# Second parts of the projection weights in a two-block transformer: computed on VectorE instead of GpSimd

## Chip, cores and metric

The kernel runs on one core of a Trainium2 chip. The metric is the device time of one execution in microseconds (us), the median of three runs of the same program. Engines are named as the profile names them: PE is TensorE (PEld its weight loads), DVE is VectorE, ACT is ScalarE, POOL is GpSimd, SP is SyncE, which here only issues DMAs. Names such as L129 are lines of the kernel before the change; the changed kernel has one line less from L394 on and two less from L1443 on, so its L470 is L471 of the kernel before.

## What is computed

Two transformer blocks over 1024 tokens of width 1024, all in float32. Cut to what matters here:

```python
def first_block(x, mem, ...):
    y = rmsnorm(h, norm_mix_g) @ w_in             # 1024 x 2560: q, k, v (512 each), conv a and g (512 each)
    att = dilated_sliding_attention(rotary(q), rotary(k), v)
    conv = conformer_conv(a, g, conv_w, ...)      # a * sigmoid(g), 31 taps per channel, layernorm, silu
    h = h + concat(att, conv) @ w_out
    ...                                           # cross attention to mem, then an MLP of 4096
def second_block(x, ...):
    z = rms_norm(x, ln1_g) @ w_in + b_in          # 1024 x 5632: q, k, v, u, y_branch, two gates
    ...                                           # neighbourhood attention; conv of 4 taps and a linear
    ...                                           # recurrence (RG-LRU) in two directions on u; MLP of 4096
```

## The kernel before

**Products in two parts.** PE multiplies in a reduced float32 form, so each float32 operand is kept as two parts. `split` (L125) makes them: ACT rounds the source into the first part `hi` (L128), and a subtraction makes the second part `lo` as source less `hi` (L129). A product is then three matmuls: hi by hi, hi by lo, lo by hi (L177 to L179 in `mm3`, L206 in `gemm_s`).

**Weights of the projections.** `w_s` (L139) fetches one chunk of 256 columns of a weight in two halves of 512 rows. Each half is a DMA of 512 KB on SP's queue (L148) into a tile `raw`, then a split into two tiles `w` of 128x1024. There are two `raw` buffers and twelve `w` buffers, so three chunks of `w` are held, and a third `raw` load waits until the `lo` of the first has been computed. The attribute `b.wlo` says who computes `lo` of these weights: `self.split(hi, lo, raw, eng=self.wlo)` at L154, where None means DVE.

**Block 1, `mix_part` (L389).** In the order of the program: the inputs are normed and transposed into `xT` (x scaled on DVE at L293, transposed on PE at L240, split at L131 and L132); then the chunks for the gate g and for a of the convolution, two halves of them (PE L206), whose product u is written by DVE (L448); then v in two chunks (n = 0 and 1) of eight 128-token tiles each, 24 matmuls of 128x256 for a tile; then q and k in four chunks. A tile of v leaves its PSUM bank by an ACT copy (L470) into a tile `t2k`, of which there are four, and goes to DRAM by an SP DMA (L471). The 31 taps of the convolution are DVE instructions on 128x1024 (L422, 30 for each of four channel groups); they stand in a background list, and `b.pump` takes some of them into the program after each tile of v (L472) and each half of a q/k chunk (L511). A scheduler then fixes one order of instructions for each engine ahead of the run, by readiness in its own model and by priority; on the chip each engine and each DMA queue works through its list in order.

**Block 2, `block2` (L1436).** Chunks of the branches y, u, q/k, v and of four gates, in a fixed list; for each of eight channel groups the background list has the small convolution, the gates and the recurrence in two directions, mostly DVE instructions on 128x1024 (L1439, L1438, L1592 to L1606). The second half of the tokens is normed at its start (L1388 to L1408, in `Front`).

**What the change touches.** L394 sets `b.wlo` to GpSimd at the start of `mix_part`, L1443 does so at the start of `block2`; each is set back to None at the end of the projections (L547, L1645). So GpSimd computes `lo` for 10 chunks in block 1 (20 tiles: g and a twice each, v twice, q/k four times) and 17 in block 2 (34 tiles). All other splits of the kernel are on DVE already.

Of the kernel before, what the change touches and what calls it, by code (L numbers as in the profile page):

```python
# [388 lines left out]
def mix_part(b):  # L389
    nc, i = b.nc, b.i  # L390
    w_in = i["w_in"][0]
    b.xk_d = b.dram.tile([4, P, 2, 2, 256], F32, name="xk_d")
    b.xv_d = b.dram.tile([4, P, 2, 2, 256], F32, name="xv_d")
    b.wlo = nc.gpsimd  # L394
    xc = i["x"][0].rearrange("(l c) d -> c l d", c=4)
    raw = [b.slot(16 + t, name="x") for t in range(NT)]
    load = lambda t: nc.sync.dma_start(out=raw[t], in_=xc[t // 2, (t % 2) * P : (t % 2 + 1) * P, :])
# [1038 lines left out]
def block2(b, h, front):  # L1436
    nc, i = b.nc, b.i
# [2 lines left out]
    turns = front.rest(h)  # L1440
    xT = front.xT

    b.wlo = nc.gpsimd  # L1443
    w_in = i["w_in_2"][0]
    b.v2_d = b.dram.tile([S, 512], F32, name="v2_d")
    b.qk2_d = b.dram.tile([4, 4, P, S], F32, name="qk2_d")
# [370 lines left out]
def build(tc, ins, out, stop=None):  # L1817
    with ExitStack() as ctx:
        b = Builder(tc, ctx, ins, out)
        b.ident = b.cpool.tile([P, P], F32, name="ident")  # L1820
        make_identity(b.nc, b.ident)
        h = mix_part(b)
        if stop not in ("mix",):
            cross_part(b, h)
        if stop not in ("mix", "cross"):
            front = Front(b)
            h = ff_part(b, h, b.g_mlp, ins["w_up"][0], ins["w_down"][0], bias_tables(b), front.work)
            b.layout(None)
        if stop not in ("mix", "cross", "ff"):
            block2(b, h, front)  # L1830
            h = merge_part(b)
        if stop is None:
            h = ff_part(b, h, b.g_ln2, ins["w_ff1_2"][0], ins["w_ff2_2"][0])
            gl = b.slot(26, name="gl")
            b.nc.sync.dma_start(out=gl, in_=ins["lnf_g_2"].partition_broadcast(P))
            final_norm(b, h, gl, out)
        else:
            for t in range(NT):
                b.nc.sync.dma_start(out=out[0, t * P : (t + 1) * P, :], in_=h[t])
# [70 lines left out]
```

## Time and profile before

| what | value |
|---|---|
| median of three runs | 3015.11 us (3013.32 to 3016.35) |
| the profiled execution | 3015.72 us, its span 3013.9 us |
| PE busy | 2895.5 us, 96% of the span |
| DVE busy | 2162.4 us, 72% |
| ACT busy | 1227.5 us, 41% |
| POOL busy | 379.2 us, 13%, of which L129 has 172.7 us in 54 instructions |
| mean granted PE clock | 0.984 of full speed |

The profile names for each instruction the engine, the line, the tiles written and read and their shape. In a row of a timeline, "x7" joins seven instructions in a row, and what stands in brackets is the idle time of that engine just ahead of the row and what ended it. SPq is SP's DMA queue. Busy time of an instruction includes the time in which it waits for data after it has started.

### The profile page before, as it was taken

The numbers are of one execution on the slowest core, as the hardware profiler recorded it, in microseconds if no ns is written. First come the engines' busy times: TensorE is split into PE (matmuls) and PEld (weight loads), VectorE is DVE, ScalarE is ACT, GpSimd is POOL, SyncE is SP. The second block draws the span as 40 slices with busy tenths as digits, with TensorE's granted clock in tenths as the row PEclk, the third lists the DMA queues.
The fourth block names the chain that finished last, engine by engine and source line by source line (L and its number), as shares of the span: only waits on it lengthen the run. The fifth ranks groups of instructions, "written<-read, shape, count | busy, mean of one in ns | idle before, by whom it ended". The sixth has DMA issues, their size and how long they took to land.

```text
span 3013.9 us, 40030 instructions
## 1 busy us (share of the span) xinstructions
PE 2895.5 (96%) x14596; PEld 2438.7 (81%) x14596; DVE 2162.4 (72%) x3889; ACT 1227.5 (41%) x2256; POOL 379.2 (13%) x411
## 2 busy tenths in 40 slices
PE   7899899999999999999999999999999999999997
PEld 5798788788887788888787788898788878888886
DVE  6997787565487776997658777554344776669976
ACT  4122566242253222444655655454211532224444
POOL 2440110000012331000021222200000011100000
PEclk9999899999999999999999999999999999999999
DMA  3135664311124767653231333567842233366522
GB/s 128 49 92 160 178 188 135 99 43 43 50 105 143 230 213 282 246 188 105 72 109 52 101 101 113 174 193 236 281 143 81 98 112 112 109 255 237 182 91 84
DMA packets 251733, 422.86 MB, mean 140 GB/s; under 512 B 27893, under 2 KB 129808, under 8 KB 251536
## 3 DMA queue, kind: packets, MB, share of 16 engines
q1 hardware_dynamic: 213040, 304.29, 31.5%
q0 software_dynamic: 30416, 101.33, 9.7%
q10 hardware_dynamic: 8080, 14.69, 1.3%
q8 instruction: 115, 1.88, 0.3%
q14 instruction: 82, 0.67, 0.1%
HBM read 310.75 MB, written 111.69 MB: 140 GB/s over the span
## 4 chain that ended last, share of the span: by engine, by line
PE 78%; DVE 9%; DMA 5%; ACT 3%; issue 2%; POOL 2%; SPq 1%; DVEq 0%; ACTq 0%; POOLq 0%
PE fd L1182 19%; PE mm L206 18%; PE ff L1009 15%; PE mm L177 5%; PE mm L179 5%; PE mm L178 5%; PE ff L992 2%; PE pv L668 2%; PE tp L734 2%; POOL w L129 1%; PE pv L1708 1%; PE tp L240 1%; DMA bt<-rpb_d 1%; ACT w L128 1%; DVE w L129 1%
## 5 line engine op out<-in xcount | busy, mean ns | idle before, releaser
L1182 PE MATMUL fd<-part,part 128*128 128x512 f32 x2688 | 616.0, 390 | 1.0 <-DVE part L129 1.0
L1182 PEld LDWEIGHTS fd<-part,part 128*128 128x128 f32 x2688 | 504.2, 188 | 110.4 <-DVE part L129 5.8
L1009 PE MATMUL ff<-x,w 128*128 128x512 f32 x2352 | 541.7, 392 | 13.8 <-ACT w L128 7.5
L1009 PEld LDWEIGHTS ff<-x,w 128*128 128x128 f32 x2352 | 443.7, 189 | 111.4 <-ACT w L128 9.2
L206 PE MATMUL mm<-xh,w 128*128 128x512 f32 x1792 | 530.7, 393 | 0.3 <-ACT lruC L1580 0.3
L206 PEld LDWEIGHTS mm<-xh,w 128*128 128x128 f32 x1792 | 336.9, 189 | 68.8 <-ACT lruC L1580 1.4
L128 ACT ACTIVATE part<-keep 128x512 fp32r<-128x512 f32 x384 | 223.8, 623 | 249.5 <-PE fd L1182 243.5
L206 PE MATMUL mm<-xl,w 128*128 128x512 f32 x896 | 316.1, 393 | 0.0
L129 DVE TENSOR_TENSOR part<-keep,part 128x512 fp32r<-128x512 f32 x384 | 250.0, 687 | 44.6 <-ACT part L128 43.9
L128 ACT ACTIVATE w<-raw 128x1024 fp32r<-128x1024 f32 (+1 forms) x132 | 134.9, 1033 | 273.5 <-PE mm L178 111.7
L129 POOL TENSOR_TENSOR w<-raw,w 128x1024 fp32r<-128x1024 f32 x54 | 172.7, 3202 | 444.7 <-ACT w L128 422.5
L206 PEld LDWEIGHTS mm<-xl,w 128*128 128x128 f32 x896 | 168.9, 189 | 33.8 <-issue 0.4
L232 DVE TENSOR_TENSOR h<-h,mm 128x512 f32<-128x512 f32 x176 | 119.8, 686 | 78.6 <-PE mm L179 78.0
L422 DVE SCALAR_TENSOR_TENSOR acc<-u,conv_wh,acc 128x1023 f32<-128x1023 f32 (+14 forms) x120 | 171.7, 1471 | 3.1 <-ACT acc L417 1.3
L177 PE MATMUL mm<-w,xh 128*128 128x256 f32 x512 | 147.9, 289 | 13.5 <-ACT t2k L470 10.3
L852 DVE TENSOR_TENSOR t2k<-ff,t2k 128x512 f32<-128x512 f32 x140 | 96.4, 688 | 82.5 <-PE ff L1009 81.1
L178 PE MATMUL mm<-w,xh 128*128 128x256 f32 x512 | 146.7, 287 | 0.0
L179 PE MATMUL mm<-w,xl 128*128 128x256 f32 x512 | 146.6, 286 | 0.0
L128 ACT ACTIVATE w<-wr 128x512 fp32r<-128x512 f32 x156 | 94.3, 630 | 119.2 <-PE ff L1009 55.5
L974 POOL DMA_DIRECT2D hid_d<-t2k x128 | 70.0, 547 | 489.2 <-DVE t2k L852 265.1
L129 DVE TENSOR_TENSOR w<-raw,w 128x1024 fp32r<-128x1024 f32 (+1 forms) x78 | 91.6, 1180 | 50.2 <-ACT w L128 50.1
L129 DVE TENSOR_TENSOR w<-wr,w 128x512 fp32r<-128x512 f32 x156 | 104.5, 687 | 15.4 <-ACT w L128 14.0
(362 smaller groups left out, 5160.0 us busy)
## 6 DMA issues: line engine op xcount, KB each, us to landing
hid_d<-t2k POOLq DMA_DIRECT2D x128, 256.0 KB, 2.9
x<-hid_d SPq DMA_DIRECT2D x128, 256.0 KB, 4.7
keep<-hid_d SPq DMA_DIRECT2D x96, 256.0 KB, 6.0
raw<-in_w_in_dram SPq DMA_DIRECT2D x38, 512.0 KB, 3.8
qk_d<-t2k SPq DMA_DIRECT2D x64, 256.0 KB, 2.5
wr<-in_w_up_dram SPq DMA_DIRECT2D x32, 512.0 KB, 4.0
keep<-in_w_down_dram SPq DMA_DIRECT2D x64, 256.0 KB, 5.3
wr<-in_w_ff_dram SPq DMA_DIRECT2D x32, 512.0 KB, 3.7
```

The lines of the kernel that those rows point to most:

```text
L128: nc.scalar.activation(hi, src, AF.Copy)
L129: (eng or nc.vector).tensor_tensor(out=lo, in0=src, in1=fp(hi), op=ALU.subtract)
L177: nc.tensor.matmul(ps, sh, mh, start=(i == 0), stop=False)
L178: nc.tensor.matmul(ps, sh, ml, start=False, stop=False)
L179: self.last = nc.tensor.matmul(ps, sl, mh, start=False, stop=(i == n - 1))
L206: self.last = nc.tensor.matmul(pj[j], a, b, start=(k == 0 and q == 0), stop=(k == nk - 1 and q == 2))
L232: self.added[t] = self.nc.vector.tensor_tensor(out=hs, in0=hs, in1=ps, op=ALU.add)
L422: nc.vector.scalar_tensor_tensor(out=acc[m][:, lo:hi], in0=u[m][:, lo + d : hi + d], scalar=w(k), in1=acc[m][:, lo:hi], op0=ALU.mult, op1= ...
L852: tt = lambda o, x, y, op: nc.vector.tensor_tensor(out=o, in0=x, in1=y, op=op)
L974: stored.append(nc.gpsimd.dma_start(out=hid[2 * c + f, :, j * 512 : (j + 1) * 512], in_=o))
L1009: b.last = nc.tensor.matmul(ps, l[:, k, :], r, start=(opens and k == 0 and q == 0), stop=(k == 3 and q == 2), skip_group_check=True)
L1182: last = nc.tensor.matmul(ps[q], l[:, sl], r, start=(c == 0 and x == 0), stop=(c == C - 1 and x == 2))
```

## The change

The two lines that hand the second parts to GpSimd are taken out, so that `b.wlo` stays None and DVE does those subtractions too. GpSimd keeps its DMA issues, its memsets and the casts of the attention.

```diff
@@ mix_part
     b.xk_d = b.dram.tile([4, P, 2, 2, 256], F32, name="xk_d")
     b.xv_d = b.dram.tile([4, P, 2, 2, 256], F32, name="xv_d")
-    b.wlo = nc.gpsimd
     xc = i["x"][0].rearrange("(l c) d -> c l d", c=4)
@@ block2
     xT = front.xT
 
-    b.wlo = nc.gpsimd
     w_in = i["w_in_2"][0]
```

The scheduler makes new lists from this. Outside three stretches (the start, block 1 from its v on, and the projections of block 2) the lists of all engines are the same, and PE's list differs in the start alone.

SP's list in block 1, from the second load of v's second chunk (raw_1247) on; raw_1512 to raw_1791 are the loads of the first two q/k chunks, v_d the stores of v. Before:

```order
L148 DMA raw_1247<-in_w_in_dram 128x4x256
L148 DMA raw_1512<-in_w_in_dram 128x4x128 x2
L148 DMA raw_1519<-in_w_in_dram 128x4x128 x2
L148 DMA raw_1784<-in_w_in_dram 128x4x128 x2
L148 DMA raw_1791<-in_w_in_dram 128x4x128 x2
L471 DMA v_d<-t2k_1008 128x256
L471 DMA v_d<-t2k_1040 128x256
```

After the change:

```order
L148 DMA raw_1247<-in_w_in_dram 128x4x256
L470 DMA v_d<-t2k_1008 128x256
L470 DMA v_d<-t2k_1040 128x256
L470 DMA v_d<-t2k_1072 128x256
L470 DMA v_d<-t2k_1106 128x256
L470 DMA v_d<-t2k_1138 128x256
L470 DMA v_d<-t2k_1170 128x256
L148 DMA raw_1512<-in_w_in_dram 128x4x128 x2
L470 DMA v_d<-t2k_1202 128x256
L148 DMA raw_1519<-in_w_in_dram 128x4x128 x2
```

The loads of two q/k chunks stood ahead of every store of v; now six stores come first and the loads stand between the later ones.

DVE's list in block 1 behind the last u of the convolution (u_799 from mm_937), which before is followed by 42 taps and then by the rotation of q and k:

```order
L448 SCALAR_TENSOR_TENSOR u_799<-th_798,mm_937 128x2x256
L422 SCALAR_TENSOR_TENSOR acc_640<-u_429,conv_wh,acc_640 128x1012
L422 SCALAR_TENSOR_TENSOR acc_1076<-u_483,conv_wh,acc_1076 128x1022
L422 SCALAR_TENSOR_TENSOR acc_640<-u_429,conv_wh,acc_640 128x1011
L422 SCALAR_TENSOR_TENSOR acc_1076<-u_483,conv_wh,acc_1076 128x1021
```

After the change 14 taps follow u_799, and then the two second parts of v's second chunk (w_1244 and w_1250):

```order
L421 SCALAR_TENSOR_TENSOR acc_1076<-u_483,conv_wh,acc_1076 128x1018
L421 SCALAR_TENSOR_TENSOR acc_640<-u_429,conv_wh,acc_640 128x1009
L421 SCALAR_TENSOR_TENSOR acc_1076<-u_483,conv_wh,acc_1076 128x1017
L129 TENSOR_TENSOR w_1244<-raw_1241,w_1243 128x1024
L421 SCALAR_TENSOR_TENSOR acc_1076<-u_483,conv_wh,acc_1076 128x1016
L129 TENSOR_TENSOR w_1250<-raw_1247,w_1249 128x1024
L421 SCALAR_TENSOR_TENSOR acc_1076<-u_483,conv_wh,acc_1076 128x1015
```

From the first tap up to w_1244 DVE's list has 61 rows: 52 taps, 5 writes of u and 4 other second parts. Behind w_1250 it has 14 taps up to the first second part of the first q/k chunk.

DVE's list at the start of block 2, in the chain of small instructions that norms the second half of the tokens (sm_13954 to sm_13956). Before:

```order
L248 TENSOR_SCALAR sm_13954<-sm_13955 128x4
L249 TENSOR_TENSOR sm_13955<-sm_13954,sm_13956 128x4
L249 TENSOR_TENSOR sm_13955<-sm_13955,sm_13954 128x4
L259 SCALAR_TENSOR_TENSOR sm_13954<-sm_13955,sm_13954 128x4
L249 TENSOR_TENSOR sm_13955<-sm_13954,sm_13956 128x4
L249 TENSOR_TENSOR sm_13955<-sm_13955,sm_13954 128x4
```

After the change:

```order
L248 TENSOR_SCALAR sm_13954<-sm_13955 128x4
L129 TENSOR_TENSOR w_14087<-raw_14084,w_14086 128x1024
L249 TENSOR_TENSOR sm_13955<-sm_13954,sm_13956 128x4
L249 TENSOR_TENSOR sm_13955<-sm_13955,sm_13954 128x4
L1438 SCALAR_TENSOR_TENSOR gy_14010<-t2k_14037,t2k_14036 128x512
L259 SCALAR_TENSOR_TENSOR sm_13954<-sm_13955,sm_13954 128x4
L249 TENSOR_TENSOR sm_13955<-sm_13954,sm_13956 128x4
L249 TENSOR_TENSOR sm_13955<-sm_13955,sm_13954 128x4
L129 TENSOR_TENSOR w_14330<-raw_14326,w_14329 128x1024
```

Two second parts of weights (w_14087 and w_14330) now stand inside the chain.

## Rows read from the trace of the kernel before

**Rows 1.** The page, part 1: each engine's busy time, its share, and its instructions.
```profile
PE 2895.5 (96%) x14596; PEld 2438.7 (81%) x14596; DVE 2162.4 (72%) x3889; ACT 1227.5 (41%) x2256; POOL 379.2 (13%) x411
```
**Rows 2.** Instructions of L129: durations in ns, least, median and longest.
```profile
L129 DVE TENSOR_TENSOR w<-raw,w x78: 676/1222/1748, 321.6 to 2300.2; 128x1024 fp32r<-128x1024 f32 x70, 128x512 fp32r<-128x512 f32 x8
...
L129 POOL TENSOR_TENSOR w<-raw,w x54: 2353/2601/20462, 12.4 to 1911.1; 128x1024 fp32r<-128x1024 f32 x54
```
**Rows 3.** Busy time by stretch: length, PE, PEld, DVE, ACT, POOL, PE clock, DMA.
```profile
120.00:180.00 60.00, 50.68 (x372) 49.18 (x371) 59.97 (x46) 12.57 (x20) 37.69 (x5) 0.91 0.17 51
...
1580.00:1640.00 60.00, 58.06 (x249) 47.42 (x248) 55.63 (x54) 39.08 (x47) 5.86 (x3) 0.97 0.11 37
```
**Rows 4.** Timeline of PE, block 1: start, duration, line, count, idle before.
```profile
138.14 0.45 PE L177 MATMUL mm<-w,xh 128*128 128x256 f32 x1 [3.06 <-DVE u L448]
...
149.03 0.58 PE L177 MATMUL mm<-w,xh 128*128 128x256 f32 x1 [6.25 <-ACT t2k L470]
...
151.76 0.38 PE L177 MATMUL mm<-w,xh 128*128 128x256 f32 x1
151.97 0.28 PE L178 MATMUL mm<-w,xh 128*128 128x256 f32 x1
152.09 0.28 PE L179 MATMUL mm<-w,xl 128*128 128x256 f32 x1
...
186.32 0.58 PE L177 MATMUL mm<-w,xh 128*128 128x256 f32 x1 [4.09 <-ACT t2k L470]
```
**Rows 5.** Timeline of ACT, v of block 1.
```profile
143.16 1.06 ACT L128 ACTIVATE w<-raw 128x1024 fp32r<-128x1024 f32 x1 [13.02 <-DMA raw<-in_w_in_dram]
...
185.90 0.37 ACT L470 COPY t2k<-mm 128x256 f32<-128x256 f32 x1 [14.72 <-DMA v_d<-t2k]
```
**Rows 6.** Waits of SP's DMA queue, 100 to 200 us: total, times, longest.
```profile
SPq L148 <- POOL w L129: 84.8, 7, 49.4
```
**Rows 7.** Timeline of POOL, v of block 1.
```profile
128.79 13.86 POOL L129 TENSOR_TENSOR w<-raw,w 128x1024 fp32r<-128x1024 f32 x2 [39.34 <-ACT w L128]
...
161.75 23.74 POOL L129 TENSOR_TENSOR w<-raw,w 128x1024 fp32r<-128x1024 f32 x2 [11.33 <-ACT w L128]
```
**Rows 8.** Timeline of DVE, the convolution of block 1.
```profile
74.54 17.30 DVE L422 SCALAR_TENSOR_TENSOR acc<-u,conv_wh,acc 128x1009 f32<-128x1009 f32 x7 [1.31 <-ACT acc L417]
...
104.32 10.79 DVE L422 SCALAR_TENSOR_TENSOR acc<-u,conv_wh,acc 128x1021 f32<-128x1021 f32 x9
...
137.00 1.08 DVE L448 SCALAR_TENSOR_TENSOR u<-th,mm 128x512 f32<-128x512 f32 x1
137.91 68.49 DVE L422 SCALAR_TENSOR_TENSOR acc<-u,conv_wh,acc 128x1012 f32<-128x1012 f32 x43
```
**Rows 9.** Timeline of DVE, the start.
```profile
40.95 2.34 DVE L248 TENSOR_SCALAR sm<-sm 128x2 int32<-128x2 int32 x1
```
**Rows 10.** Timeline of PE, the start.
```profile
44.72 0.44 PE L240 MATMUL tp<-ident,x 128*128 128x128 f32 x2 [2.05 <-DVE xl L132]
```
**Rows 11.** Timeline of DVE, block 2.
```profile
1503.12 1.23 DVE L1388 TENSOR_TENSOR h<-h,gf 128x1024 f32<-128x1024 f32 x1 [1.66 <-ACT junk L1387]
...
1507.10 2.98 DVE L1388 TENSOR_TENSOR h<-h,gf 128x1024 f32<-128x1024 f32 x1 [2.15 <-ACT junk L1387]
...
1879.44 1.22 DVE L1438 TENSOR_TENSOR lruC<-lruC,lruA 128x1024 f32<-128x1024 f32 x1
...
1889.51 3.42 DVE L1438 TENSOR_TENSOR lruC<-lruC,lruA 128x1024 f32<-128x1024 f32 x1
```
**Rows 12.** Timeline of PE, block 2.
```profile
1524.07 0.33 PE L240 MATMUL sc<-ident,h 128*128 128x128 f32 x1 [0.94 <-DVE h L1408]
...
1616.09 0.65 PE L177 MATMUL mm<-w,w 128*128 128x512 f32 x1 [1.94 <-ACT lruA L1580]
...
1657.54 0.80 PE L177 MATMUL mm<-w,w 128*128 128x512 f32 x1 [2.79 <-ACT t2k L1471]
```
**Rows 13.** Timeline of ACT, block 2.
```profile
1655.85 1.06 ACT L128 ACTIVATE w<-raw 128x1024 fp32r<-128x1024 f32 x1 [2.29 <-DMA raw<-in_w_in_dram]
```

## The prediction

> **What bounds the kernel now.** I read the page's busy times first. PE works 2895.5 us, 96% of the span [rows 1], so an edit on other engines can win only where PE idles or runs at a low clock, and can lose wherever its new owner makes PE wait. Then I read the groups of L129: the same 128x1024 subtraction takes DVE 1.222 us in the median, and GpSimd between 2.353 and 20.462 us [rows 2]. Next come the stretches. Between 120 and 180 us DVE is busy 59.97 us of 60, PE only 50.68, and PE's mean granted clock is 0.91 [rows 3]: of the two levels, 1.2 and 2.4 GHz, it had the lower one for part of the time. That is v of block 1.
>
> The chain of causes there is read from four engines. GpSimd's second parts come out in pairs that last 13.86 and 23.74 us [rows 7], though two at its shortest would be 4.7. They lie beside the convolution's taps on DVE, and the taps are long there too: 9 taps from 104.32 on take 10.79 us, 1.20 each, at a time when GpSimd is idle (39.34 us up to 128.79) [rows 7, 8], whereas 7 taps from 74.54 on take 17.30, and 43 from 137.91 on take 68.49 [rows 8]. So the two engines hold each other up when both read SBUF. The late second part keeps a `raw` buffer, and SP's queue stands at the next `raw` load: 7 waits of 84.8 us in all, the longest 49.4 [rows 6]. Behind it in SP's list stand the stores of v. ACT therefore waits 13.02 us for a `raw` load and 14.72 us for a `v_d` store to release its `t2k` [rows 5], and PE idles 3.06, 6.25 and 4.09 us [rows 4], 13.40 in all. The first is put down to u, a write that DVE reached at 137.00 only, behind taps [rows 8]. After each such pause PE restarts slowly: from 149.03 to 151.76 thirteen matmuls are 0.21 us apart, and after that 0.12 (151.97 to 152.09) [rows 4]. The other two pauses are followed by 16 and 14 slow ones; 43 times 0.09 is about 4 us.
>
> **The change part by part.**
>
> *What DVE gets.* 54 subtractions at 1.22 us: 20 in block 1 (24.4 us) and 34 in block 2 (41.5 us). *What DVE loses.* The time in which GpSimd held it up. In block 1: 17.30 less 7x1.20 is 8.9; 68.49 less 43x1.20 is 16.9 [rows 8]; five rows at the start like the one of 2.34 us for two columns at 40.95 [rows 9] come to about 9, and one at 218 us to 1.6. That makes 36 us, more than the 24.4 it gets. In block 2, 19 rows are longer than the same instruction elsewhere, from 1507.10 (2.98 us against 1.23) to 1889.51 (3.42 against 1.22) [rows 11], about 2 us each, 39 in all, against 41.5. So DVE's load falls by some 12 us in block 1 and is unchanged in block 2.
>
> *A: v of block 1.* PE reaches v at 138.14 - 3.06 (idle) - three tiles of 24 matmuls at 0.12 (8.64) = 126.4 [rows 4]. On DVE, w_1244 has 61 rows ahead of it from 74.54 on: 56 (52 taps and 4 second parts) at 1.20 and 5 u at 0.91 (137.00 to 137.91, [rows 8]) make 71.8, so it starts at 146.3 and ends at 147.5, and w_1250 about 2.5 us later, as a tap stands between. The last of the u, u_799, stands 14 taps (16.8 us) and itself ahead of w_1244: it starts at about 128.6, well ahead of the 135.1 at which PE ran out before. PE needs w_1244 after eight tiles of 2.88 us, at 149.4, and w_1250 about 1.5 us later: margins of 2 us and 1 us. For q/k's first chunk 14 taps stand behind w_1250, so its second part is there at about 168, and PE asks for it at 126.4 + 16x2.88 = 172.5. SP now has six stores ahead of the next `raw` load, so no `t2k` waits behind a load. All three pauses go, and the slow restarts with them: **-13.4 - 4 = -17.4 us**. The margins are thin, and I set **+2 us** for small new pauses there (from 0, if my 1.20 holds, to 12, if the taps stay long; see the first rival).
>
> *B: the start.* PE waits 2.05 us for an xl at 44.72 [rows 10], which comes behind the long row of 40.95 [rows 9]. In exchange four second parts of 1.22 us stand in DVE's list ahead of or between the xl. The two bounds are -4 us (the long rows go, the new ones hide) and +3 (new ones in the chain, long ones hidden anyway); I take **-2**, since each long row lost about 2.1 and each new one costs 1.22.
>
> *C: block 2.* The norm chain of the second half held two of the long rows, beside the 1507.10 one; now two second parts stand in it. PE's wait of 0.94 and 0.33 behind `h` at 1524.07 [rows 12] goes: -1.3. At 1657.54 PE waits 2.79 us for ACT [rows 12], which waited 2.29 us for a `raw` load [rows 13], the same buffer chain as in block 1; of it I expect 1.1 back. The 1.94 us at 1616.09 [rows 12] come from the recurrence, whose DVE time does not change. **-2.4**; bounds -10 (all the pauses of block 2 that DVE or ACT end) and the third rival.
>
> *At nothing:* GpSimd's 172.7 us, of which nothing else waits but what is named; its loads; the casts of the attention, which have no second part beside them. ACT's work is the same. The DMAs are the same in number.
>
> **Sum.** -17.4 + 2 - 2 - 2.4 = -19.8 against the profiled 3015.72 us: 2995.9. The median of the runs is 0.6 us lower: **2995 us**, 0.7% faster. A measurement of this kernel can tell about 0.2%, 6 us.
>
> **A rule weighed.** DVE is full between 120 and 180 us [rows 3], and still the 9 taps beside an idle GpSimd run in 1.20 us each and those beside a busy one in 1.59 [rows 8]. The Trainium skill, "Perfetto Trace Analysis", section "Optimizing Scalar/DVE Operations", says that handing work to ScalarE or even GpSimd may make sense when DVE is saturated, and also that between GpSimd and DVE it might not help, as they share an SBUF read port. By its first half the change puts 24.4 us on the full engine and the pauses of v grow; by its second half it gives back 36 first. The rows speak for the second half, and the first is the first rival's outcome.
>
> **The rivals.**
>
> *1. The taps don't get shorter (0.10).* If what lengthens them is not GpSimd, for instance their operands or ACT, then a tap takes what it took before: 42 of them and 4 u between 74.54 and 137.00 [rows 8], so (62.5 - 3.6) / 42 = 1.40 each. w_1244 then starts after 56x1.40 + 5x0.91 = 83 us, at 157.5, and ends at 158.7, 9.3 us too late; w_1250 adds 1.2 and the slow restart 1.3. Of 17.4 us some 6 come back, and B and C stay what they were: about 3009. Against it: the 10.79 us for 9 taps just where GpSimd idles. For it: these rows are few, and within the 43 no row says which tap was held.
>
> *2. The pauses belong to the buffers (0.07).* There are two `raw`, four `t2k` and SP's one list, whoever computes. The first q/k load is even asked for later now. If the pauses only move to another load or store, the time is 3013 to 3015. Against it: the waits of SP's queue are put down to GpSimd by name [rows 6], and the stores now precede the loads.
>
> *3. Slower: the recurrence of block 2 (0.11).* DVE is busy 55.63 us of 60 between 1580 and 1640 [rows 3], and PE's 1.94 us at 1616.09 wait through ACT for it [rows 12]. If GpSimd's pieces ran in DVE's gaps and the long rows lay off the path, 34x1.14 to 34x1.22 us (39 to 41.5) come onto the chain with no relief: at worst 3015.1 - 17.4 + 39 = 3037. It turns the sign once more than about 20 us of that reach PE. Against it: only 1.94 of PE's pauses there are DVE's now, and the long rows are as many as the new work.
>
> **How the numbers follow.** The forecast has 0.72, the rivals 0.10, 0.07 and 0.11. The range reaches down to no pause in A, B as taken, and C at its 10 us (3015.1 - 17.4 - 2 - 10 = 2985.7, so 2986), and up to the first rival (3009); outside lie the second and third and a few hundredths of the forecast. The first rival lies at the edge of 0.2%; half of it counts as the same. Faster 0.72 + 0.05 = 0.77, same 0.07 + 0.05 = 0.12, slower 0.11.
>
> **What would show it.** Right: no wait of SP's queue for L129 of POOL; no pauses of PE at v of block 1, and a granted clock near 1.0 in 120 to 180 us; taps of 1.20 each; POOL's busy time near 379 - 173 = 206 us, DVE's within 20 of before; no row of 2.3 us for a small tile at the start. Wrong in A: a pause at PE's eighth tile of v that ends with w_1244. Wrong in C: new pauses of PE behind lruA, or behind ACT waiting for DVE, between 1480 and 1900 us.

## The result, and the profile after

The changed kernel takes 2983.26 us in the median of three runs (2978.47 to 2986.51); the ratio to the kernel before is 0.9882 (95% interval 0.9867 to 0.9898). It is faster, as forecast, by 31.9 us where 20 were forecast, and lies just below the range of 2986 to 3009.

The page after, part 1; the row that answers to it is in [rows 1]:

```profile
PE 2883.3 (97%) x14596; PEld 2430.3 (82%) x14596; DVE 2146.0 (72%) x3943; ACT 1228.6 (41%) x2256; POOL 206.9 (7%) x357
```

GpSimd lost 172 us, DVE gained 54 instructions and is still busy 16 us less, and PE needs 12 us less for the same 14596 matmuls. Where the time went shows when both traces are cut at four instructions of ScalarE, the same four in both: a split of a weight chunk as the convolution's taps begin, a split of transposed q/k near the end of block 1's projections, a split just ahead of block 2's, and a copy of probabilities as block 2's attention begins. The counts of matmuls in brackets agree but for a missing record or two. Busy time by those five stretches, columns as in [rows 3], before:

```profile
0.00:77.30 77.30, 55.15 (x251) 43.88 (x252) 48.43 (x128) 37.75 (x72) 23.13 (x25) 0.98 0.37 125
77.30:252.40 175.10, 161.58 (x1116) 152.32 (x1115) 164.47 (x139) 35.84 (x65) 66.18 (x16) 0.96 0.24 76
252.40:1475.40 1223.00, 1179.46 (x6125) 994.59 (x6125) 905.78 (x1981) 504.22 (x1073) 136.40 (x229) 0.98 0.46 148
1475.40:1964.70 489.30, 477.26 (x2282) 399.03 (x2281) 350.49 (x367) 282.85 (x362) 107.26 (x58) 0.99 0.34 108
1964.70:3013.90 1049.20, 1022.05 (x4829) 848.86 (x4827) 693.25 (x1277) 366.82 (x688) 46.26 (x84) 0.99 0.48 158
```

After:

```profile
0.00:70.00 70.00, 53.03 (x251) 42.72 (x252) 44.02 (x135) 38.18 (x72) 7.58 (x18) 1.00 0.41 138
70.00:227.40 157.40, 156.70 (x1116) 147.98 (x1115) 153.44 (x152) 36.28 (x64) 1.53 (x2) 1.00 0.27 84
227.40:1454.60 1227.20, 1180.02 (x6126) 994.80 (x6125) 905.60 (x1981) 504.57 (x1074) 136.37 (x229) 0.98 0.45 148
1454.60:1932.70 478.10, 471.55 (x2280) 395.78 (x2279) 349.93 (x401) 283.00 (x361) 15.18 (x24) 1.00 0.35 110
1932.70:2981.50 1048.80, 1021.98 (x4829) 848.98 (x4828) 693.03 (x1277) 366.60 (x688) 46.26 (x84) 0.99 0.47 158
```

The length less PE's busy time is PE's idle time; PE's matmuls are the same, so a change of its busy time is the granted clock.

| stretch | in all | idle | clock | forecast |
|---|---|---|---|---|
| start | -7.3 | -5.2 | -2.1 | -2 |
| v, q, k of block 1 | -17.7 | -12.8 | -4.9 | -15.4 |
| up to block 2 | +4.2 | +3.6 | +0.6 | 0 |
| block 2, projections | -11.2 | -5.5 | -5.7 | -2.4 |
| the rest | -0.4 | -0.3 | -0.1 | 0 |

In v of block 1 no pause is left. The timeline of DVE there answers to [rows 8]: taps of 1.20 us throughout, and w_1244, the second part at 138.43, starts 71.2 us after the first tap at 67.28 (forecast 71.8).

```profile
67.28 2.58 DVE L421 SCALAR_TENSOR_TENSOR acc<-u,conv_wh,acc 128x1009 f32<-128x1009 f32 x2 [1.32 <-ACT acc L416]
...
121.82 16.68 DVE L421 SCALAR_TENSOR_TENSOR acc<-u,conv_wh,acc 128x1015 f32<-128x1015 f32 x14
138.43 1.21 DVE L129 TENSOR_TENSOR w<-raw,w 128x1024 fp32r<-128x1024 f32 x1
```

The waits of SP's queue for L129 from 75 to 180 us answer to [rows 6] and are short now; it mostly waits for the copies of v, which is its normal work:

```profile
SPq L470 <- ACT t2k L469: 69.1, 14, 42.9
SPq L148 <- DVE w L129: 16.7, 10, 2.8
```

In block 2 the pauses at 1616, 1710, 1712 and 1764 us are gone. The two of 1.03 and 1.54 us behind h, at its start, stay (1.02 and 1.53). Of the later ones one is left that matters; it answers to the one of 2.79 us in [rows 12]. PE's timeline, and ScalarE's ahead of it:

```profile
1629.93 0.50 PE L177 MATMUL mm<-w,w 128*128 128x512 f32 x1 [2.71 <-ACT t2k L1469]
```
```profile
1625.40 1.06 ACT L128 ACTIVATE w<-raw 128x1024 fp32r<-128x1024 f32 x1 [4.24 <-DMA raw<-in_w_in_dram]
1628.24 1.06 ACT L128 ACTIVATE w<-raw 128x1024 fp32r<-128x1024 f32 x1 [1.78 <-DMA raw<-in_w_in_dram]
1629.21 0.67 ACT L1469 ACTIVATE t2k<-mm,cols 128x512 f32<-128x512 f32 x1
```

The copy that PE waits for stands behind two splits that wait for their loads.

What a pause of block 2 can cost besides itself is read from short windows behind three of them, before:

```profile
1616.30:1619.60 3.30, 3.30 (x9) 2.37 (x9) 1.24 (x2) 3.30 (x6) 0.00 (x0) 0.50 0.18 71
1657.30:1660.60 3.30, 2.93 (x6) 1.70 (x6) 1.72 (x1) 3.24 (x5) 2.57 (x2) 0.50 0.74 236
1711.90:1715.20 3.30, 3.28 (x8) 2.60 (x9) 1.23 (x1) 3.30 (x6) 1.77 (x1) 0.50 0.20 46
```

Each is at the lower of the two clock levels, 1.2 GHz, and so loses about half its length. A fourth such stretch stands behind the pause of 1.54 us at 1479, and none behind that at 1764. After the change only the pause at 1630 is followed by one.

### The profile page after: what moved, and what is told of

It reads as the page before. It is cut to its first block, busy times and chain, and to the rows that moved or that the text cites. A ratio compares the mean times of both kernels' runs of the same rounds, so it can differ in the third digit from the quotient of the medians.

```text
span 2981.5 us, 40017 instructions
## 1 busy us (share of the span) xinstructions
PE 2883.3 (97%) x14596; PEld 2430.3 (82%) x14596; DVE 2146.0 (72%) x3943; ACT 1228.6 (41%) x2256; POOL 206.9 (7%) x357
## 4 chain that ended last, share of the span: by engine, by line
PE 79%; DVE 11%; DMA 4%; ACT 3%; issue 2%; SPq 0%; POOL 0%; DVEq 0%; ACTq 0%; POOLq 0%
PE mm L206 20%; PE fd L1181 19%; PE ff L1008 15%; PE mm L177 5%; PE mm L179 5%; PE mm L178 5%; DVE acc L421 3%; PE ff L991 2%; PE pv L667 2%; PE tp L733 2%; PE pv L1706 1%; PE tp L240 1%; DVE w L129 1%; DMA bt<-rpb_d 1%; DMA raw<-in_w_in_dram 1%
## 5 line engine op out<-in xcount | busy, mean ns | idle before, releaser
L129 DVE TENSOR_TENSOR part<-keep,part 128x512 fp32r<-128x512 f32 x384 | 249.2, 682 | 44.7 <-ACT part L128 44.0
L129 DVE TENSOR_TENSOR w<-raw,w 128x1024 fp32r<-128x1024 f32 (+1 forms) x132 | 157.4, 1196 | 84.2 <-ACT w L128 68.2
L421 DVE SCALAR_TENSOR_TENSOR acc<-u,conv_wh,acc 128x1016 f32<-128x1016 f32 (+14 forms) x120 | 148.0, 1268 | 2.5 <-ACT acc L416 1.3
L129 DVE TENSOR_TENSOR w<-wr,w 128x512 fp32r<-128x512 f32 x156 | 104.4, 686 | 16.9 <-ACT w L128 15.4
L725 ACT ACTIVATE pr<-sc,sm 128x256 f32<-128x256 f32 (+1 forms) x192 | 97.4, 509 | 39.7 <-DVE sm L722 29.8
L1067 DVE TENSOR_TENSOR keep<-keep,keep 128x512 f32<-128x512 f32 x160 | 105.0, 681 | 0.0
```

The lines of the kernel that those rows point to most:

```text
L129: (eng or nc.vector).tensor_tensor(out=lo, in0=src, in1=fp(hi), op=ALU.subtract)
L421: nc.vector.scalar_tensor_tensor(out=acc[m][:, lo:hi], in0=u[m][:, lo + d : hi + d], scalar=w(k), in1=acc[m][:, lo:hi], op0=ALU.mult, op1= ...
L725: b.nc.scalar.activation(pr, sc, AF.Exp, scale=-1.0, bias=nm, accum_out=den)
L1067: tt = lambda o, x, y, op: nc.vector.tensor_tensor(out=o, in0=x, in1=y, op=op)
```

## The experiments

The theory behind them: GpSimd and DVE hold each other up when both read SBUF, and that, in three places, was what PE waited for. The rivals: only the lateness of GpSimd's own results counted; or the buffers and SP's queue did.

**Block 1 alone, and block 2 alone.** Each keeps GpSimd in the other block; against the changed kernel, for the first:

```diff
 def block2(...)
+    b.wlo = nc.gpsimd
```

> VectorE computes the second parts in block 1, GpSimd still in block 2. Theory (the gain has two places, read from the shift of ACT's instructions between the two traces: 25 us by the end of the q/k chunks of block 1, of which 4 are given back by 1120 us, and 11 in block 2): 20.9 us faster than before, 2994 us (2990 to 2998), with block 2's pauses of TensorE and their slow clock as before. Rival (block 2 gained only the 2.4 us of the prediction, the rest is block 1's): about 2986.

Measured: 2995.81 us, ratio 0.9924 (0.9910 to 0.9938), 22.9 us below the before of its chip (3018.75). Block 2 keeps its pauses, 1.94 us in the longest wait behind the recurrence.

> VectorE computes the second parts in block 2, GpSimd still in block 1. Theory: 11 us faster, 3004 us (3001 to 3008): the pauses at 1616, 1710 and 1763 us go, each with a stretch of 3.4 us at half clock. Rival (block 2's recurrence has no room, the gain is block 1's): 3013 to 3015.

Measured: 3007.37 us, 0.9962 (0.9950 to 0.9975), 11.4 us. The two add up to the change, 34.3 us against 31.9, within the scatter of the runs. In its trace block 2 has little more than the pauses of the changed kernel (2.73 and 1.03 us), and v of block 1 keeps pauses of 11.50 and 3.89 us. The lists of PE, DVE, GpSimd and SP in block 1 are those of the kernel before, which had 3.06, 6.25 and 4.09 there: in [rows 8] four long taps stand behind the last u, here four fell ahead of it. So the same lists give these pauses in more than one form (timelines of DVE and PE):

```profile
126.00 19.25 DVE L422 SCALAR_TENSOR_TENSOR acc<-u,conv_wh,acc 128x1017 f32<-128x1017 f32 x9
145.17 1.05 DVE L448 SCALAR_TENSOR_TENSOR u<-th,mm 128x512 f32<-128x512 f32 x1
```
```profile
146.27 0.58 PE L177 MATMUL mm<-w,xh 128*128 128x256 f32 x1 [11.50 <-DVE u L448]
```

**Only the convolution's inputs, and only v, q and k.** `b.wlo` is switched where `v_d` is made: in the first kernel from None to GpSimd (and block 2 keeps GpSimd), in the second from GpSimd to None.

```diff
+    b.wlo = nc.gpsimd
     b.v_d = b.dram.tile([S, 512], F32, name="v_d")
```

> VectorE computes the second parts of the four chunks of the convolution's inputs alone (8 tiles); v, q and k of block 1 and all of block 2 stay with GpSimd. Theory (the start and v are two gains, 7 us and 18 us): the waits of 1.87, 1.85 and 2.05 us and the half clock after them go, and v keeps pauses of about 13 us: 5 to 9 us faster than before. Rival (v's pauses come only from the 8.9 us by which VectorE's taps are late before v begins): v's pauses go too, 20 us faster.

Measured: 3009.85 us, 0.9973 (0.9962 to 0.9983), 8.4 us. The theory holds: the start is won, and PE keeps 5.95 and 5.25 us of pauses in v.

```profile
135.91 0.58 PE L177 MATMUL mm<-w,xh 128*128 128x256 f32 x1 [5.95 <-ACT t2k L470]
...
175.36 0.58 PE L177 MATMUL mm<-w,xh 128*128 128x256 f32 x1 [5.25 <-ACT t2k L470]
```

> VectorE computes the second parts of v, q and k of block 1 alone; the four chunks of the convolution's inputs and block 2 stay with GpSimd. Theory (two places in block 1 that add: 8 us at the start as measured, the rest here): the start as before, VectorE about 9 us late at the first tap stretch, so that v's second chunk, which had a margin of 2 us, is late by up to 7: 8 to 14 us faster than before. Rival (the margins hold all the same): 17 us faster.

Measured: 3002.91 us, 0.9956 (0.9941 to 0.9970), 14.2 us. The number is the theory's, or nearly, but not its reason: v has no pause at all. One of 4.13 us has come at the first transpose of q and k instead:

```profile
198.33 0.47 PE L240 MATMUL tp<-ident,y 128*128 128x128 f32 x1 [4.13 <-DVE y L494]
```

**GpSimd beside, with nobody using its result.** The lists of PE, DVE and ACT are those of the changed kernel.

```diff
-            self.split(hi, lo, raw, eng=self.wlo)
+            self.split(hi, lo, raw)
+            if self.wlo is not None:
+                flat = fp(hi).rearrange("p k n -> p (k n)")
+                for a, b in ((0, 384), (384, 768), (768, 1024)):
...
+                    self.wlo.tensor_tensor(out=idle[:, : b - a], in0=flat[:, a:b], in1=flat[:, a:b], op=ALU.subtract)
```

> The changed kernel with the same lists on TensorE, VectorE and ScalarE, and beside each second part that VectorE computes in the projections GpSimd subtracts the first part from itself into a buffer that nobody reads, in three pieces of 384, 384 and 256 columns. Nobody waits for GpSimd's result. Theory (the two engines hold each other up when both read SBUF): VectorE's taps and small instructions become long again, by 0.8 to 1 us for each piece that lies beside a full VectorE; 60 pieces in block 1 are up to 50 us on a VectorE that had a margin of 2, so pauses of TensorE at v come back: 3000 to 3025 us. Rival (the gain came only from results that were late on GpSimd, not from contention): 2983 to 2987 us, and taps of 1.20 us.

Measured: 3018.99 us, 1.0001 (0.9992 to 1.0009): the whole gain is gone, though DVE still computes every second part. On DVE a second part that takes 1.21 us alone, or a tap that takes 1.27, takes 1.84 beside a piece (timeline of DVE):

```profile
151.76 1.21 DVE L129 TENSOR_TENSOR w<-raw,w 128x1024 fp32r<-128x1024 f32 x1
152.89 1.84 DVE L427 SCALAR_TENSOR_TENSOR acc<-u,conv_wh,acc 128x1016 f32<-128x1016 f32 x1
154.65 1.84 DVE L129 TENSOR_TENSOR w<-raw,w 128x1024 fp32r<-128x1024 f32 x1
```

And PE pauses again, here for DVE directly, and at the recurrence of block 2 (timeline of PE):

```profile
153.03 0.39 PE L183 MATMUL mm<-w,xh 128*128 128x256 f32 x1 [2.89 <-DVE w L129]
...
213.16 0.48 PE L245 MATMUL tp<-ident,y 128*128 128x128 f32 x1 [9.76 <-DVE y L498]
...
1618.64 0.69 PE L182 MATMUL mm<-w,w 128*128 128x512 f32 x1 [2.39 <-ACT lruA L1585]
```

GpSimd still held something up itself: at 157.01 ScalarE's rounding of a weight waits 9.42 us for a buffer that a piece reads, and loads of block 2 wait 31.0 us on SP's queue for it, 18.4 before. In block 1 no pause of PE hangs on that: the next is at 213.16, and DVE is not idle in between. The one at 1618.64 comes through the recurrence on DVE.

**GpSimd beside, filling with zeros.** First with a `memset` in place of the subtraction; in a second kernel the copy of two columns of `hi` in the diff's first line, ahead of the fills, spreads them out.

```diff
+                self.wlo.tensor_copy(out=idle[:, :2], in_=flat[:, :2])
...
-                    self.wlo.tensor_tensor(out=idle[:, : b - a], in0=flat[:, a:b], in1=flat[:, a:b], op=ALU.subtract)
+                    self.wlo.memset(idle[:, : b - a], 0.0)
```

> The same as the kernel in which GpSimd subtracts beside, but GpSimd fills the same buffers with zeros in place of the subtraction, so it writes SBUF and reads nothing. Theory (reading two inputs is what collides): 2983 us within 4, taps of 1.20 us. Rival (any work of GpSimd on SBUF holds VectorE up): as long as the kernel that subtracts beside, or a part of the way to it.

Measured: 3005.16 us, 0.9957 (0.9945 to 0.9970), a part of the way to the kernel before, as the rival had it, but not by taps that are long. Fills wait for nothing and so ran in one row at the start, 48 of them in 15.66 us (timeline of GpSimd), and one small instruction of DVE was held for 10.51 us (timeline of DVE):

```profile
13.46 15.66 POOL L159 MEMSET pt<- 128x384 f32 x48
```
```profile
16.96 1.22 DVE L129 TENSOR_TENSOR w<-raw,w 128x1024 fp32r<-128x1024 f32 x1
18.09 0.15 DVE L254 TENSOR_TENSOR sm<-sm,sm 128x2 f32<-128x2 f32 x1
18.64 10.51 DVE L273 TENSOR_SCALAR sm<-sm 128x2 f32<-128x2 f32 x1 [0.39 <-ACT t2k L272]
```

The instructions with two inputs at 16.96 and 18.09 were not held by the same fills; the one at 18.71, just behind the held one, ended with it. PE then waited 15.57 us in place of 5.23. In block 2 another row, of 66 fills, held a single-input instruction on 128x4 for 5.68 us (1498.47), and of the 11.2 us won there 4.4 are left.

> The changed kernel with the same lists on all engines but GpSimd, which beside each second part copies two columns of the first part and then fills the same buffers with zeros as the earlier kernel did; the copy makes the fills wait for the first part, so that they are spread out as the subtractions were and no longer run in one row at the start. Theory (what cost 13 to 22 us there was one small instruction of VectorE with a single input, held for 10.5 us by fills in a row; instructions with two inputs are not held by fills): within 5 us of the changed kernel, which is 1.2% below before, and taps of 1.20 us. Rival (fills collide like subtractions): 15 us slower than the changed kernel or more.

Measured: 2985.51 us, 0.9891 (0.9878 to 0.9904), the changed kernel's time, with taps of 1.20 us (timeline of DVE):

```profile
122.11 16.70 DVE L428 SCALAR_TENSOR_TENSOR acc<-u,conv_wh,acc 128x1015 f32<-128x1015 f32 x14
138.72 1.22 DVE L129 TENSOR_TENSOR w<-raw,w 128x1024 fp32r<-128x1024 f32 x1
```

So it is GpSimd's reading beside DVE, and not its work as such, that makes taps and second parts long; fills cost only where a row of them held a single-input instruction.

**GpSimd in four pieces.** The lists are those of the kernel before.

```diff
+                for q in range(4):
+                    eng.tensor_tensor(out=lo[:, q], in0=src[:, q], in1=fp(hi)[:, q], op=ALU.subtract)
```

> The kernel before, with GpSimd computing each second part in four pieces of 256 columns; all other lists are the same. Theory (an operation of either engine blocks the other for its whole length, seen as 0.62 us for each piece of 384 columns and about 2 us for a whole one of 1024): VectorE's long rows shrink to about 0.5 us each and get several times as many, the sum stays within a third of 34 us in block 1, and the time within 6 us of before. Rival (each turn has a price of its own): slower by 6 us or more. Rival (a short piece lets VectorE through and its small instructions no longer wait long): faster by 6 us or more.

Measured: 3018.13 us, 1.0003 (0.9994 to 1.0013). Up to 260 us, DVE's rows beside GpSimd's work, each less the median of its kind in the changed kernel, are 0.46 us longer in place of about 2, but 63 of them in place of 18: 29 us in all against 35. The size of a piece settles nothing.

**The queue and the buffers.** The stores of v on ScalarE's queue; then three `raw` buffers for two, paid for by one of the twelve `w` (`NW = 11`), with the kernel before and with the changed one.

```diff
-            nc.sync.dma_start(out=b.v_d[...], in_=st)
+            nc.scalar.dma_start(out=b.v_d[...], in_=st)
```

> The kernel before, with the stores of v issued on ScalarE's queue in place of SyncE's, so that they no longer stand behind the raw loads that wait for GpSimd; VectorE's and GpSimd's lists are the same. Theory (the queue that stands still is one of three causes of v's pauses): the pause of 4.09 us, which ended with a copy that waited 14.72 us for a store, goes with its half clock; that of 6.25 us gets shorter or ends with the second part of v's second chunk; that of 3.06 us behind u stays: 4 to 9 us faster. Rival 1 (the queue is all of it): 15 us faster or more. Rival 2 (only late second parts count): within 3 us of before.

Measured: 3013.91 us, 0.9990 (0.9981 to 0.9999). The pause of 4.09 us shrinks to 1.02, and v is 3.9 us shorter. In place of the other two (9.31) stands one of 11.51 behind u on DVE. That is not the queue's doing, as the kernel with block 2 alone has the same form with the queue of before. So the theory was right on the third pause; of the second this run shows only that with the queue freed DVE is late all the same.

```profile
147.76 0.58 PE L177 MATMUL mm<-w,xh 128*128 128x256 f32 x1 [11.51 <-DVE u L448]
```

```diff
-            self.rpool = pool("raw", 2)
+            self.rpool = pool("raw", 3)
```

> The kernel before (GpSimd computes the second parts) with three raw buffers in place of two, and eleven w buffers in place of twelve, which pays for the third. Theory (the engines hold each other up; the buffers only pass the delay on): VectorE's long rows stay (some 35 us in block 1 and 38 in block 2), v keeps most of its pauses: within 8 us of before. Rival (the pauses belong to the two raw buffers): v's pauses and those of block 2 behind a raw load go: 17 us faster or more.

Measured: 3011.39 us, 0.9977 (0.9966 to 0.9987). Again PE waits for u, 11.44 us, and 4.86 later, and v is as long as before. The third buffer, less what the twelfth `w` was worth, is 6 us over the whole kernel, not 17. It does not free the queue, which between 100 and 200 us still waits 75.4 us for GpSimd (84.8 before).

> The changed kernel with three raw buffers and eleven w buffers. Theory (the one pause left in block 2 that counts, 2.71 us at 1630 us with its half clock, comes from a copy that stands on ScalarE behind two raw loads): it goes, 2 to 4 us faster than the changed kernel (ratio to before 0.987). Rival (eleven w buffers make later chunks wait for TensorE to free one): slower than the changed kernel by 3 us or more.

Measured: 2974.72 us (2973.10 to 2978.99), 0.9856 (0.9843 to 0.9870). The pause at 1630 is gone; what is left behind ScalarE in block 2 is 0.52 and 0.62 us. It is the fastest version of all: its median is 8.5 us below the changed kernel's, on another chip, where the before was 2 us slower. Of the 8.8 us between the two traces 4.7 lie in block 2; 4.4 lie between the blocks, where the next kernel, with two buffers and on the same chip, is as short, so they are not put down to the buffer. Its lists differ from the changed kernel's in many other places too.

**The casts on ScalarE.** `nc.scalar.copy` for GpSimd's `tensor_copy` into `qb`.

> The changed kernel with the eight casts of a head's queries (128x1024, 1.04 us each), the last work of GpSimd on SBUF beside VectorE, on ScalarE. Theory (a cast held only two of VectorE's rows, by 0.53 us each, and ScalarE ends many waits of the attention): within 6 us of the changed kernel, rather slower. Rival (GpSimd beside VectorE always costs several times what is seen): 4 us faster or more.

Measured: 2981.24 us, 0.9874 (0.9860 to 0.9887): not to be told from the changed kernel.

## Why the prediction was right and wrong

**A** was right. The three pauses of [rows 4] went with their slow clock, -17.7 against -17.4, and the account of DVE's list was good to 0.6 us. The +2 for thin margins was not needed: only 0.70 us came back, at the first transpose of q and k. That DVE, and not the queue, was the first cause, is shown by the kernel that took the stores off the queue and still had 11.5 us behind u, and by the subtractions beside, which brought pauses back though DVE made every second part.

**B** was mis-sized, -2 against -7.3. The bounds, -4 and +3, do not hold it either. Of PE's three waits of 1.87, 1.85 and 2.05 us it counted the last; all three went, as a long row stood ahead of each (2.29 us at 28.07, 2.89 at 38.15, 2.34 at 40.95), while the new second parts, which it set against them, cost PE 0.8 us at one place. The clock, for which it had no term, made up the other 2.1.

**C failed.** It said that at 1616.09 the wait comes "from the recurrence, whose DVE time does not change". DVE's busy time in block 2 indeed did not change (350.49 and 349.93 us). But a sum does not say where in the chain the time stands. Before, two long rows fell among the recurrence's own instructions ahead of that wait (timeline of DVE):

```profile
1596.08 3.36 DVE L1439 SCALAR_TENSOR_TENSOR lruE<-lruB,lruA 128x1024 f32<-128x1024 f32 x1
...
1605.89 3.49 DVE L1438 TENSOR_TENSOR t2k<-t2k,t2k 128x512 f32<-128x512 f32 x2
```

After:

```profile
1571.16 1.20 DVE L1438 SCALAR_TENSOR_TENSOR lruE<-lruB,lruA 128x1024 f32<-128x1024 f32 x1
...
1574.62 1.21 DVE L129 TENSOR_TENSOR w<-raw,w 128x1024 fp32r<-128x1024 f32 x1
...
1579.83 1.28 DVE L1437 TENSOR_TENSOR t2k<-t2k,t2k 128x512 f32<-128x512 f32 x2
...
1583.24 1.19 DVE L129 TENSOR_TENSOR w<-raw,w 128x1024 fp32r<-128x1024 f32 x1
```

The chain gives up 4.4 us and takes in two second parts, 2.3 us; the 2.1 us left over are about the pause of 1.94 that is gone. Three more second parts, between 1535 and 1549 us, go into time in which DVE had been idle. The kernel with GpSimd beside has those second parts and the collisions as well: its pause there is back, 2.39 us, and block 2 as long as before.

And C had no term for the clock, which A had: of 11.2 us, 5.7 are the low clock behind pauses. Some 1.6 of these are luck: behind the pause of 1.54 us at 1479 the clock fell before, and behind the same pause of 1.53 at 1459 it did not after; in the kernel with the spread fills, whose list on PE is the same, it did, and block 2 won 9.7.

The 1.3 us that C expected at the norm chain came. The pauses at 1710, 1712 and 1764 it had only in its bound of -10. What of them goes through `raw` loads and what through DVE stays open: with GpSimd and three buffers those at 1710 and 1712 are still 0.56 and 1.66 us, but that kernel's lists differ there. The one pause that C did expect to shrink, 2.79 us, stayed (2.71): a third buffer takes it away in the changed kernel, though not where GpSimd computes (3.62 us, the copy then waiting for a store).

**The range** took at its bottom no pause in v, -2 at the start and -10 in block 2. Start and block 2 went 5.3 and 1.2 us beyond that, and the 4.2 us of the next paragraph bring the time back to 2.7 below 2986.

**Not foreseen:** 4.2 us were given back between the two blocks, where the lists are equal. Most of it is not the change's. The kernels that leave block 1 as it was (block 2 alone, the stores moved, GpSimd in four pieces) are 2.1 to 2.8 us longer there than the trace of before as well; of those with the changed block 1, the kernel with the spread fills is 2.5 us longer, the one with block 1 alone 0.8, and the one with the casts on ScalarE 0.2 shorter. So this stretch differs from run to run, as the whole time does (8 us over three runs), and the trace of before was short there. Why it varies is open.

**The rivals.** The first fell: taps are 1.20 us. The second is what the queue and buffer kernels tested: 4 and 6 us, not 17; one more buffer is not all of them, so what still more would do is not shown. The third fell too, by e2's 11 us in block 2 alone. Of the rule on a full DVE the second half held: the full engine took its subtractions back and the kernel got faster, and reading beside it on GpSimd, with DVE as full as before (60.00 us of 60 between 120 and 180), took the whole gain away. The Trainium skill, "SBUF — State Buffer", section "Who interferes with whom", says that a DVE instruction with two SBUF inputs collides with GpSimd instructions that read SBUF and not with those that only write it. The traces agree: a second part took 1.84 us beside subtractions and 1.22 beside fills.

## What to carry to other kernels

Work moved to an idle GpSimd is not free for DVE: put beside the time it takes what DVE's rows gain in length while it runs, and look for them in the chains that PE waits on, not in DVE's busy time. Add to a pause of PE the slow clock that may stand behind it, at every place and not only where it was first seen, as a range: the same pause had it in one trace and not in another. Beside a queue that stands still an engine may be late as well: free the queue, and see which wait is left. Read one list in more than one trace before a change in the form of its pauses is put down to an edit.

## What the runs showed of the hardware

Fills of GpSimd, which read nothing, left DVE's two-input instructions alone (1.22 us, 0.15 us) but held one single-input TENSOR_SCALAR on 128x2 for 10.51 us, until a row of fills at 0.33 us each had ended. The instruction did not get in between two fills, and neither did one on 128x4 in block 2 of the same run (5.68 us). But three on 128x1024 there, from 1516.09 on, did get in beside fills and took 0.98 to 1.24 us in place of 0.75; what decides it is not shown.

Between subtractions of GpSimd and a full DVE the turns mostly alternate: a piece of 384 columns makes a tap 0.57 us longer and a second part 0.63. GpSimd does not always get its turn: one piece, at 145.81, took 7.84 us, while five taps and a second part of DVE ran at their usual length.
